# One filling slab of a state-space stage queued behind the stage's last product

## The chip, the cores and the metric

The kernel runs on one core of a Trainium2 chip. The metric is the device time of one execution in microseconds (us). Engines are named as in the profile: PE is TensorE (PEld its weight loads), DVE is VectorE, ACT is ScalarE, POOL is GpSimd, SP is SyncE, which issues the DMAs. All products are of float32 data, split into a high and a low part, so that one logical product is three on PE (high by high, low by high, high by low).

## What is computed

One decoder layer over 1024 tokens of width 1024 with two token mixers side by side, cut here to what matters:

```python
h = rmsnorm(x, norm_w) * (1 + scale) + shift               # scale, shift, gate from c
z_ssm, xbc, dt_raw, q, k, v, z_att, f_logit, g_logit = split(h @ w_in)
# state-space branch: conv and silu on xbc, then 8 chunks of 128 tokens, 16 heads of 64
y = diag(C B^T * L) @ x  +  C @ state  +  d_skip * x         # state runs from chunk to chunk
y_ssm = rmsnorm(y * silu(z_ssm), ssm_norm_w)
# attention branch: 8 heads of 128, causal softmax with a forgetting bias
y_att = softmax(q k^T * s + f_i - f_j) @ v * silu(z_att)
merged = g_ssm * (y_ssm @ w_proj_ssm) + g_att * (y_att @ w_proj_att)
out = rmsnorm(x + gate * (merged @ w_out), final_norm_w)
```

## The kernel before

The kernel is written with a tile framework. The program is traced in source order; then a planner in the compiler lays out a fixed queue for each engine. It steps through a simulated timeline and, whenever an engine is free, gives it the instruction of highest priority whose inputs are planned to be there. Priority is source order, raised for blocks under `tc.high_priority`. Tiles of one tag share a fixed number of buffers (`bufs`); a tile gets its buffer when its first write is placed, and gives it back after its last use. On the chip the queues run as laid out.

The stages around the change:

- **Projection stage** (up to about 500 us of the span): `h` lies in SBUF as `hh`, `hl` (high and low part). Column slabs of `w_in` are multiplied with it and stored to DRAM.
- **State-space stage** (lines 637 to 801, pool `sd`): for each of four groups of heads (`qd`) and each half of the sequence (`hf`), `ssd_half` runs four chunks `c`. A chunk has, on PE, two transposes (L698), three products for the new state (L718), twelve for the part inside the chunk (`yd`, L735) and four for the part from the state (`yo`, L746 and L747). DVE and ACT form the decay matrix and carry the state `st32` from chunk to chunk. After a half, two rows of `y` are finished (L779, L780) and their squares are added into `sacc` (L782 to L785). `ssd_half` has high priority (offset 300).
- **Filling slabs** (`fill`, L762, and `FILL`, L55): parts of the projection that attention needs later, put into this stage so that PE has something to do while the chain of the state waits. They are three slabs of v and seven of q and k (`SPILL`). The list of the last group is `[1, 3, 6, 7, 8]`: `fill[8]` is `qk_spill("k", 5)`, the k of head 5, called **k5** here. A slab is `c_slab` (L115): two weight units, each loaded (L85), cast (L98) and subtracted (L99), then two halves of 24 products (L111 to L113) into one PSUM tile `mm` each. Tag `mm` has three buffers (L74), `wh` and `wl` five each (L92, L95), `wr` four. A half of k5 is read out by L191 into a tile `qt` of tag `ev` (four buffers for the whole kernel, L80), and the slab is stored by L192.
- **End of the stage**: eight products per half of `sacc` with a column of ones (L791) give the sums of squares (`rps`), then L794, L796 (POOL), L798, L800 and a store to `r_scr`. When the last reader of the pool `sd` is done, the pools of attention (`at`, `atp`) take its memory.
- **Attention** (L974 to L1088): `attend(h)` has high priority (offset 1000). The q and k of head 0 are loaded from the spilled ones (L990); those of head 1, **q1** and **k1**, are not spilled. `qk_slab(1)` computes them with `c_slab` into the same three `mm` buffers and reads them out (L980, L981, L985, L986) into tiles of `at`. `u_scaled` (L810) loads, scales and stores the eight rows of y again through `ev` tiles, six of them after head 0. The load of k5 comes with head 5 (L990).
- After that, early products of the state-space branch (L913 to L915, L964 to L966) fill the rest of attention, then the output products follow.

Of the kernel before, what the change touches and what calls it, by code (L numbers as in the profile page):

```python
# [51 lines left out]
WPREP = {1: [('ps', 0)], 2: [('ps', 1)], 3: [('ps', 2)], 6: [('ps', 3), ('pa', 0)], 8: [('pa', 1)], 10: [('pa', 2), ('g', 0)], 12: [('pa', 3), ('g', 2), ('g', 3)], 11: [('g', 1)], 13: [('G', 0)], 15: [('o', 0)], 16: [('o', 1)], 17: [('o', 2)], 18: [('o', 3)]}  # L52
PREP = (6, 1, 0, 0, 0, 0, 0, 0, 1)
APRI, SPRI = 1000, 300
FILL = [[], [0, 2], [4, 5, 9], [1, 3, 6, 7, 8]]  # L55
PAIRS = [(G0 + 4, G0 + 5), (XB0 + 8, XB0 + 9), (G0 + 6, G0 + 7), (XB0, XB0 + 1), (Z0, Z0 + 1), (XB0 + 2, XB0 + 3),
         (Z0 + 2, Z0 + 3), (XB0 + 4, XB0 + 5), (G0 + 8, G0 + 9), (XB0 + 6, XB0 + 7), (G0 + 10, G0 + 11)]
# [8 lines left out]
def build(ctx, tc, t):  # L66
    nc = tc.nc
    V, A, G, PE, SP = nc.vector, nc.scalar, nc.gpsimd, nc.tensor, nc.sync
# [269 lines left out]
    def v_slab(pair, dtf=None):  # L338
        vt = []

        def evac(tb, ps):
            per = ps.shape[1]
            g, i = tb // 4, tb % 4
            if i == 0:
                vt.append(ev("vt")[:, :1024].rearrange("p (i c) -> p i c", i=4))
            A.copy(out=vt[g][:, i:i + per, :], in_=ps[:, :, 0:256])
            if dtf is not None:
                V.tensor_copy(out=dtf[:, tb:tb + per, :], in_=ps[:, :, 256:280])  # L348
            if i + per == 4:
                SP.dma_start(out=v_scr[pair][g], in_=vt[g])  # L350

        if dtf is not None:
            with tc.issue_after(was["last"].ins):
                t_slab([t["w_v0"][u] for u in range(4)], 280, hh, hl, evac)
        else:
            t_slab([t["w_v"][pair - 1, u] for u in range(4)], 256, hh, hl, evac)
# [280 lines left out]
    with tc.tile_pool(name="sd", bufs=1, side="right") as sd, \  # L637
            tc.tile_pool(name="sdp", bufs=1, space=PSUM) as sdp:

        def sp():  # L640
            return sdp.tile([P, 512], F32, tag="sp", bufs=4, name="sp")
# [8 lines left out]
        cl = [sd.tile([P, S], F32R, name=f"cl{g}") for g in range(2)]  # L650
# [12 lines left out]
        for c in range(NC):  # L663
            tk = slice(c * P, (c + 1) * P)
# [5 lines left out]
            if c < NC - 1:  # L670
# [4 lines left out]
                A.copy(out=bt[:, c, 0].rearrange("p (q d) -> p q d", q=2), in_=b4[:, 0::3])  # L675
                A.copy(out=bt[:, c, 1].rearrange("p (q d) -> p q d", q=2), in_=b4[:, 1:3])

        def ssd_half(qd, hf, xs, ys, st32, sn):

            g = qd // 2  # L680
            gs = slice(g * 64, (g + 1) * 64)
            for c in range(4 * hf, 4 * hf + 4):
                tk = slice(c * P, (c + 1) * P)
# [30 lines left out]
                so = sn  # L714
# [22 lines left out]
                if c > 0:  # L737
                    eb = sd.tile([P, 2, P], F32, tag="eb", bufs=2, name="eb")
                    for z in range(2):
                        SP.dma_start(out=eb[z * 64:(z + 1) * 64],  # L740
                                     in_=e_scr[r0:r0 + 4].rearrange("(r two) l -> two r l", two=2)[z:z + 1]
                                     .broadcast_to([64, 2, P]))
                    yo = sp()
                    for i in range(2):
                        ps_ = slice(i * P, (i + 1) * P)
                        PE.matmul(yo[:, ps_], lhsT=so[:, ps_], rhs=ch[g][:, tk], start=True, stop=False)  # L746
                        PE.matmul(yo[:, ps_], lhsT=so[:, ps_], rhs=cl[g][:, tk], start=False, stop=True)  # L747
                    V.tensor_tensor(out=ys[:, :, th], in0=yo[:, 0:256].rearrange("p (r l) -> p r l", r=2), in1=eb,
                                    op=ALU.mult)
                    for z in range(2):  # L750
                        V.tensor_tensor(out=ys[half[z], :, th], in0=yd[z], in1=ys[half[z], :, th], op=ALU.add)
                else:
                    for z in range(2):
                        A.copy(out=ys[half[z], :, th], in_=yd[z])
            return sn

        def qk_spill(n, h):
            evac, store = qk_out(n, h)
            c_slab(t["w_c"], (Q0 if n == "q" else K0) + h, hh, hl, evac)
            store()  # L760

        fill = [lambda p=p: v_slab(p) for p in (1, 2, 3)] + [lambda a=a: qk_spill(*a) for a in SPILL]  # L762
        sacc = sd.tile([P, S], F32, name="sacc")
        for qd in range(4):
            st32, sn = sd.tile([P, 256], F32, tag="st32", bufs=1, name="st32"), None
            for hf in range(2):
                hs = slice(hf * 512, (hf + 1) * 512)
                xs = [sd.tile([P, 512], F32, tag="xs", bufs=5, name="xs") for _ in range(2)]
                for i in range(2):
                    SP.dma_start(out=xs[i], in_=x_scr[2 * qd + i][:, hs])  # L770
                ys = sd.tile([P, 2, 512], F32, tag="ys", bufs=2, name="ys")
                with tc.high_priority(offset=SPRI):
                    sn = ssd_half(qd, hf, xs, ys, st32, sn)
                for i in range(2):
                    j = 2 * qd + i
                    zt = sd.tile([P, 512], F32, tag="zt", bufs=2, name="zt")
                    SP.dma_start(out=zt, in_=z_scr[j][:, hs])
                    y = ys[:, i]
                    V.scalar_tensor_tensor(out=y, in0=xs[i], scalar=dskip[:, j:j + 1], in1=y, op0=ALU.mult, op1=ALU.add)  # L779
                    V.tensor_tensor(out=y, in0=y, in1=zt, op=ALU.mult)  # L780
                    if j == 0:
                        A.activation(out=sacc[:, hs], in_=y, func=AF.Square)  # L782
                    else:
                        A.activation(out=zt, in_=y, func=AF.Square)
                        V.tensor_tensor(out=sacc[:, hs], in0=sacc[:, hs], in1=zt, op=ALU.add)  # L785
                    SP.dma_start(out=u_scr[j][:, hs], in_=y)
            for f in FILL[qd]:
                fill[f]()
        rps = sp()
        for tb in range(8):  # L790
            PE.matmul(rps[:, 2 * tb:2 * tb + 1], lhsT=sacc[:, tb * P:(tb + 1) * P], rhs=ones[:, 0:1],  # L791
                      start=True, stop=True)
# [457 lines left out]
```

## Time and profile before

| what | us |
|---|---|
| median of 3 runs (lowest to highest) | 1224.31 (1223.64 to 1227.98) |
| the profiled execution, its own time | 1224.89 |
| its span in the profile | 1223.2 |
| state-space stage, last product L747 starts | 715.68 |
| first product of attention, L1030 | 729.09 |

The profile's page has the busy time of each engine; the windows view has it for any stretch of time, with the granted clock of PE (1.00 is full speed) and the share of time in which the DMA engines were busy. The timeline view lists instructions in order of their start; in brackets stands the time for which the engine sat idle before one and what ended it.

### The profile page before, as it was taken

Reading aid. Unit: us, or ns where it says so; the run is one execution under the profiler, and the core shown is the slowest. Engines: PE = TensorE matmul, PEld = TensorE weight load, DVE = VectorE, ACT = ScalarE, POOL = GpSimd, SP = SyncE. Lnnn points to the kernel's source line nnn. Section 1 sums busy time; section 2 is a strip of 40 time slices with the busy share of each in tenths; the row PEclk is TensorE's granted clock in tenths of the full one; section 3 lists DMA queues with packets and bytes.
Section 4 is the critical chain, followed back from the end, with each engine's and each line's share of the span. In section 5 each row is a group of like instructions: output and inputs, shape, how many; then the busy total and the mean of one; then the engine's idle time right before and its main releaser. Section 6 shows DMA issues by size and latency. Waiting matters only on the chain.

```text
span 1223.2 us, 18391 instructions
## 1 busy us (share of the span) xinstructions
PE 1162.6 (95%) x6206; PEld 976.3 (80%) x6206; DVE 957.2 (78%) x1950; ACT 626.5 (51%) x1252; POOL 88.3 (7%) x152
## 2 busy tenths in 40 slices
PE   4899999999999999999999989999989998999997
PEld 2788888788877878998987777888877886788876
DVE  6956689788987685589999986664677968989967
ACT  5554444453443334777676633454456644354465
POOL 2000000000000000000000002222322220000001
PEclk9899999999999999999999999999999999999999
DMA  8765543655485665646545658422255526965333
GB/s 351 274 233 184 185 154 93 231 189 189 129 309 167 224 224 200 202 152 223 187 150 186 199 213 294 155 92 73 87 176 195 182 77 239 326 190 182 104 96 147
DMA packets 109018, 228.26 MB, mean 187 GB/s; under 512 B 12362, under 2 KB 20220, under 8 KB 107900
## 3 DMA queue, kind: packets, MB, share of 16 engines
q1 hardware_dynamic: 108924, 227.09, 55.1%
q8 instruction: 49, 0.80, 0.3%
q14 instruction: 45, 0.37, 0.1%
HBM read 159.14 MB, written 67.90 MB: 186 GB/s over the span
## 4 chain that ended last, share of the span: by engine, by line
PE 66%; DVE 15%; DMA 12%; issue 4%; ACT 3%; POOL 1%; SPq 0%; DVEq 0%; POOLq 0%; ACTq 0%
PE pp L497 4%; PE pp L499 4%; PE pp L500 4%; PE pv L1061 4%; PE mm L497 3%; PE mm L499 3%; PE mm L112 3%; PE mm L500 3%; PE mm L113 3%; PE lg L1030 3%; PE mm L111 3%; DMA ab<-a_scr 3%; PE tp L1051 2%; PE mm L915 2%; PE mm L913 2%
## 5 line engine op out<-in xcount | busy, mean ns | idle before, releaser
L98 ACT CAST wh<-wr 128x512 fp32r<-128x512 f32 (+1 forms) x214 | 130.8, 619 | 171.7 <-DMA wr<-w_c 35.0
L99 DVE TENSOR_TENSOR wl<-wr,wh 128x512 fp32r<-128x512 f32 (+1 forms) x214 | 145.5, 686 | 44.9 <-ACT wh L98 44.6
L112 PE MATMUL mm<-hl,wh 128*128 128x512 f32 x288 | 116.4, 404 | 1.9 <-DVE hl L306 1.9
L111 PE MATMUL mm<-hh,wh 128*128 128x512 f32 x288 | 115.7, 406 | 0.1
L113 PE MATMUL mm<-hh,wl 128*128 128x512 f32 x288 | 115.1, 400 | 0.0
L136 PE MATMUL mm<-wh,hh 128*128 128x256 f32 (+1 forms) x256 | 73.8, 289 | 2.4 <-DVE tmp L348 2.4
L137 PE MATMUL mm<-wl,hh 128*128 128x256 f32 (+1 forms) x256 | 74.4, 292 | 0.0
L138 PE MATMUL mm<-wh,hl 128*128 128x256 f32 (+1 forms) x256 | 73.6, 288 | 0.0
L1036 ACT ACTIVATE pr<-pr,sm 128x1024 f32<-128x1024 f32 (+3 forms) x64 | 49.9, 780 | 44.8 <-DVE sm L1035 38.1
L1054 ACT CAST pth<-tp 128x512 fp32r<-128x512 f32 (+1 forms) x80 | 42.5, 542 | 53.5 <-PE tp L1051 43.7
L1031 DVE CUSTOM_DVE_ANT_0 pr<-lg,fb 128x512 f32<-128x512 f32 (+1 forms) x96 | 51.3, 551 | 18.7 <-PE lg L1030 13.2
L112 PEld LDWEIGHTS mm<-hl,wh 128*128 128x128 f32 x288 | 55.0, 191 | 13.2 <-DVE hl L306 3.3
L113 PEld LDWEIGHTS mm<-hh,wl 128*128 128x128 f32 x288 | 54.9, 191 | 10.3
L111 PEld LDWEIGHTS mm<-hh,wh 128*128 128x128 f32 x288 | 54.5, 191 | 10.5 <-ACT hh L305 0.7
L690 ACT ACTIVATE ab<-ab,acs 128x128 f32<-128x128 f32 x128 | 41.2, 391 | 37.7 <-DMA ab<-a_scr 34.1
L1055 DVE TENSOR_TENSOR ptl<-tp,pth 128x512 fp32r<-128x512 f32 (+1 forms) x80 | 49.9, 630 | 10.2 <-ACT pth L1054 9.8
L1039 POOL TENSOR_SCALAR pr<-pr,sm 128x1024 f32<-128x1024 f32 (+3 forms) x64 | 52.2, 816 | 78.2 <-DVE sm L1038 65.4
L98 ACT CAST sh<-sr 128x512 fp32r<-128x512 f32 x57 | 33.9, 619 | 42.3 <-DVE sr L479 31.3
L796 POOL TENSOR_TENSOR fl<-fl,mhalf 128x8 f32<-128x8 f32 x1 | 1.6, 1648 | 699.0 <-DVE fl L794 699.0
L136 PEld LDWEIGHTS mm<-wh,hh 128*128 128x128 f32 x256 | 48.8, 191 | 2.8 <-DVE tmp L348 2.6
L138 PEld LDWEIGHTS mm<-wh,hl 128*128 128x128 f32 x256 | 49.1, 192 | 0.0
L137 PEld LDWEIGHTS mm<-wl,hh 128*128 128x128 f32 x256 | 48.9, 191 | 0.2
(406 smaller groups left out, 3485.5 us busy)
## 6 DMA issues: line engine op xcount, KB each, us to landing
wr<-w_c SPq DMA_DIRECT2D x116, 256.0 KB, 3.7
wa<-w_ada SPq DMA_DIRECT2D x8, 1024.0 KB, 11.4
g_scr<-gt SPq DMA_DIRECT2D x16, 512.0 KB, 4.2
ab<-a_scr SPq DMA_DIRECT2D x32, 256.0 KB, 3.9
gt<-g_scr SPq DMA_DIRECT2D x32, 256.0 KB, 4.0
wr<-w_ps SPq DMA_DIRECT2D x28, 256.0 KB, 2.7
wr<-w_pa SPq DMA_DIRECT2D x28, 256.0 KB, 2.7
wr<-so SPq DMA_DIRECT2D x28, 256.0 KB, 2.7
```

The source lines that it names most:

```text
L98: A.copy(out=hi[:, :n], in_=raw[:, :n])
L99: eng.tensor_tensor(out=lo[:, :n], in0=raw[:, :n], in1=f32(hi[:, :n]), op=ALU.subtract)
L111: PE.matmul(ps, lhsT=hi[:, cs], rhs=xh[k][:, hs], start=(k == 0), stop=False)
L112: PE.matmul(ps, lhsT=hi[:, cs], rhs=xl[k][:, hs], start=False, stop=False)
L113: PE.matmul(ps, lhsT=lo[:, cs], rhs=xh[k][:, hs], start=False, stop=(k == 7))
L136: PE.matmul(o, lhsT=xh[k][:, ts], rhs=hi[:, cs], start=(k == 0), stop=False)
L137: PE.matmul(o, lhsT=xh[k][:, ts], rhs=lo[:, cs], start=False, stop=False)
L138: PE.matmul(o, lhsT=xl[k][:, ts], rhs=hi[:, cs], start=False, stop=(k == 7))
L497: PE.matmul(ps, lhsT=f[0][:, w], rhs=xh[:, hs], start=(first and k == 0), stop=False, skip_group_check=True)
L499: PE.matmul(ps, lhsT=f[0][:, w], rhs=xl[:, hs], start=False, stop=False, skip_group_check=True)
L500: PE.matmul(ps, lhsT=f[1][:, w], rhs=xh[:, hs], start=False, stop=(k == 3), skip_group_check=True)
L1039: G.tensor_scalar(out=pr[:, :n], in0=pr[:, :n], scalar1=sm[:, 1:2], scalar2=0.5, op0=ALU.mult, op1=ALU.mult)
```

## The change

The planner is told that every PE instruction of `fill[8]` (k5) comes behind the last `yo` product of the state-space stage in PE's queue. `last_mm["ssd"]` holds the product traced last (L747 of group 3, second half, chunk 7, second pair); `tc.issue_after` adds for each PE instruction traced in its block an edge to that product: order of issue only, no wait for its result. The loads, casts, subtractions, read-outs and the store of k5 get no such edge. Nothing else changes.

```diff
@@ -52,6 +52,7 @@
 APRI, SPRI = 1000, 300
+KEPT = 8
 FILL = [[], [0, 2], [4, 5, 9], [1, 3, 6, 7, 8]]
@@ -675,6 +676,8 @@
+        last_mm = {}
+
         def ssd_half(qd, hf, xs, ys, st32, sn):
@@ -744,7 +747,8 @@
                         PE.matmul(yo[:, ps_], lhsT=so[:, ps_], rhs=ch[g][:, tk], start=True, stop=False)
-                        PE.matmul(yo[:, ps_], lhsT=so[:, ps_], rhs=cl[g][:, tk], start=False, stop=True)
+                        last_mm["ssd"] = PE.matmul(yo[:, ps_], lhsT=so[:, ps_], rhs=cl[g][:, tk], start=False,
+                                                   stop=True)
@@ -785,7 +789,11 @@
             for f in FILL[qd]:
-                fill[f]()
+                if f == KEPT:
+                    with tc.issue_after(last_mm["ssd"].ins):
+                        fill[f]()
+                else:
+                    fill[f]()
```

## The prediction

> **What bounds the kernel now.** I read the page first, for which engine carries the end, then the windows around the stage's end, then the timelines of PE, DVE, ACT and SP there.
>
> ```profile
> span 1223.2 us, 18391 instructions
> PE 1162.6 (95%) x6206; PEld 976.3 (80%) x6206; DVE 957.2 (78%) x1950; ACT 626.5 (51%) x1252; POOL 88.3 (7%) x152
> PE 66%; DVE 15%; DMA 12%; issue 4%; ACT 3%; POOL 1%; SPq 0%; DVEq 0%; POOLq 0%; ACTq 0%
> ```
>
> PE is busy for 1162.6 of 1223.2 us. The change adds and removes no PE work, so it acts through PE's 60.6 us of idle time and through the clock: a microsecond is lost when PE stands still where it now works, and won back only where it later finds work in what is now an idle stretch. The windows (columns: length, then busy time and count of PE, PEld, DVE, ACT, POOL, then granted clock, DMA share, GB/s) show where idle time lies:
>
> ```profile
> 640.00:703.40 63.40, 59.66 (x377) 49.25 (x377) 59.46 (x145) 41.10 (x100) 0.00 (x0) 1.00 0.61 196
> 703.40:715.90 12.50, 12.37 (x85) 10.18 (x82) 11.60 (x29) 3.07 (x6) 0.00 (x0) 1.00 0.67 228
> 715.90:724.40 8.50, 8.50 (x43) 7.07 (x43) 6.98 (x13) 1.86 (x3) 0.00 (x0) 1.00 0.37 126
> 724.40:770.00 45.60, 39.17 (x201) 32.30 (x200) 30.98 (x61) 18.77 (x33) 11.00 (x15) 0.96 0.77 271
> 770.00:1223.00 453.00, 432.12 (x2236) 362.79 (x2234) 345.40 (x754) 232.09 (x459) 70.80 (x122) 0.99 0.47 155
> ```
>
> From 703.4 to 724.4 PE is never short of work. DVE, with 11.60 of 12.50 us, is the engine that paces the state's chain there. So the gap that a kept slab could fill, from the last product to the sums of squares, is full already. What fills it is in the next fence:
>
> ```profile
> 715.68 0.28 PE L747 MATMUL sp<-cl,sn 128*128 128x128 f32 x1
> 715.80 1.00 PE L791 MATMUL sp<-ones,sacc 128*128 128x1 f32 x8
> 716.66 0.47 PE L111 MATMUL mm<-hh,wh 128*128 128x512 f32 x1
> 716.97 0.39 PE L112 MATMUL mm<-hl,wh 128*128 128x512 f32 x1
> 717.20 0.39 PE L113 MATMUL mm<-hh,wl 128*128 128x512 f32 x1
> ...
> 724.15 0.39 PE L113 MATMUL mm<-hh,wl 128*128 128x512 f32 x1
> 724.38 0.95 PE L791 MATMUL sp<-ones,sacc 128*128 128x1 f32 x8
> ```
>
> Whose products are these? k5's read-outs and stores tell (L191 reads out a half, L192 stores a slab):
>
> ```profile
> 692.36 0.60 ACT L191 ACTIVATE qt<-mm 128x512 f32<-128x512 f32 x1
> 702.77 0.59 ACT L191 ACTIVATE qt<-mm 128x512 f32<-128x512 f32 x1
> 689.30 0.32 SPq L192 DMA_DIRECT2D q_scr<-qt  x1
> 691.66 0.42 SPq L812 DMA_DIRECT2D ut<-u_scr  x1
> 703.39 0.45 SPq L192 DMA_DIRECT2D k_scr<-qt  x1
> ```
>
> q7 is stored at 689.30 and k5, the last spilled slab, at 703.39: k5's two halves were read out at 692.36 and 702.77. So the filling products after 702.4 are q1 and k1, of head 1 of attention. A count on tile `mm` (same columns):
>
> ```profile
> 703.40:715.90 12.50, 9.16 (x36) 6.47 (x36) 0.00 (x0) 0.00 (x0) 1.00 0.67 228
> 715.90:724.40 8.50, 7.74 (x33) 6.13 (x33) 0.00 (x0) 0.00 (x0) 1.00 0.37 126
> 728.21 1.07 ACT L980 ACTIVATE qh<-mm 128x512 fp32r<-128x512 f32 x2
> 731.79 0.49 PE L111 MATMUL mm<-hh,wh 128*128 128x512 f32 x1
> ```
>
> 36 and 33 products, and one triple just before 703.4, are 72 = 3 x 24: q1's two halves and k1's first, one in each of the three `mm` buffers. Then it stops. They can be read out only into attention's tiles, which come with the end of the pool `sd` (L980 at 728.21), and the next filling product is at 731.79. **The reader should see two things**: three buffers are all that attention's slabs can take ahead of time, and a later instruction in the source does take a buffer ahead of an earlier one (the load of `ut`, L812, was issued at 691.66 into a tile of tag `ev`, before k5's own `ev` tile was written at 692.36, though k5 comes first in the source).
>
> **The change part by part.** k5's 48 products lose their place between about 686 and 702.4. They may go behind 715.68. Loads, casts and subtractions of k5's two units stay early (no edge binds them).
>
> *What takes the places.* q1 is ready at that time. Its products move up, then k1's first half: the 72 products of above. From 686 to 715.7 there are 48 + 39 = 87 places, so the 72 are used up about 15 products before the last product, near 709.5. By then all three `mm` buffers hold q1 and k1, which nobody can read out before `sd` closes. **k5 finds no buffer behind the last product**, and PE has no filling until q1 is read out. That is my forecast: the slab that was kept for the gap isn't in the gap.
>
> *What is deferred.* One product takes 0.23 us in a row (716.97 to 717.20), so 48 x 0.23 = 11.1 us of PE work pass from before 724.4 to attention. It is behind attention's own work in priority; its reader, the load for head 5, is far:
>
> ```profile
> 889.95 0.32 SPq L990 DMA_DIRECT2D qt<-k_scr  x1
> ```
>
> *What becomes earlier.* The sums of squares wait for DVE:
>
> ```profile
> 716.55 0.69 DVE L99 TENSOR_TENSOR wl<-wr,wh 128x512 fp32r<-128x512 f32 x1
> 721.03 0.68 DVE L99 TENSOR_TENSOR wl<-wr,wh 128x512 fp32r<-128x512 f32 x1
> 721.63 1.48 DVE L785 TENSOR_TENSOR sacc<-sacc,zt 128x512 f32<-128x512 f32 x2
> ```
>
> `sacc` is complete at 723.11, the products that read it start at 724.38: 1.27 us go, since no filling stands in front. The two subtractions in that tail are for units of later slabs; with k5's two units held, five `wh`/`wl` buffers don't suffice for them, and they drop out of the tail. Both lie between steps of the chain; I count 1.0 of their 1.37 us. The chain before gains at most DVE's idle time, 12.50 - 11.60 = 0.9 us; I take 0.5. Together attention starts 2.8 us earlier (bounds 1.3 and 3.5).
>
> *The clock.* After idle stretches the granted clock falls in this trace:
>
> ```profile
> 724.40:727.50 3.10, 1.11 (x10) 0.92 (x8) 1.23 (x2) 2.14 (x3) 1.65 (x1) 1.00 0.17 70
> 727.50:729.00 1.50, 0.08 (x1) 0.00 (x0) 1.50 (x4) 1.50 (x3) 0.00 (x0) 0.86 0.75 289
> 729.00:731.80 2.80, 2.71 (x7) 2.16 (x8) 2.80 (x4) 0.76 (x2) 0.59 (x2) 0.50 1.00 392
> ```
>
> PE works 1.19 of 4.6 us there and then runs at 0.50. With an empty gap from about 716.7 to 722 the eight records of L791 behind it run at half clock: 0.8 us more (their 0.84 us between starts once again). The slow stretch after 729 is there already and stays. By the Trainium skill, "TensorE: Matmul & The Clock Gate", Part 1, an idle window of about 3.4 us halves the clock, and a busy one of 3.4 us restores it. The trace's 0.50 agrees with the half; were the gap charged one whole slow window, 3.4 / 2 = 1.7 us, an estimate from that page, the sum would end 0.9 us higher.
>
> *What is won back.* The deferred work fills later idle time, if that idle time is for want of filling. Candidates:
>
> ```profile
> 906.69 0.47 PE L111 MATMUL mm<-hh,wh 128*128 128x512 f32 x1
> 923.03 0.51 PE L913 MATMUL mm<-bh,wh 128*128 128x512 f32 x1
> 910.00:920.00 10.00, 6.08 (x24) 4.14 (x24) 7.98 (x26) 5.70 (x12) 3.75 (x5) 0.82 0.97 332
> 1000.00:1020.00 20.00, 17.32 (x120) 15.07 (x119) 10.98 (x33) 9.40 (x22) 6.01 (x12) 1.00 0.12 39
> 1020.00:1040.00 20.00, 18.21 (x75) 13.35 (x73) 19.15 (x32) 10.09 (x18) 0.00 (x0) 1.00 1.02 356
> ```
>
> The hole at 910 to 920 lies between the last slab's products (last L111 at 906.69) and the first early product (L913 at 923.03), while DMA is full (0.97); it moves with the last slab and isn't filled. The end of attention, 1000 to 1020, lacks filling: 2.7 us. From 1020 to 1040 PE waits for loads (DMA 1.02): 1.8 us more. I take both, 4.5. The bounds are nothing and 11.1, all of it, since 724.4 to 1223 has 6.4 + 20.9 us of idle time.
>
> *The rest.* k5's store of 512 KB moves from 703.39 to some 20 us after the slab's new place; on SP it stands among the loads of `ut`, and k5's `ev` tile takes one of four buffers from their cycle. PE waits little for that cycle, so I cost it at nothing; with the cover gone it is one wait as below, 1.0 us.
>
> ```profile
> 768.33 0.36 PE L1061 MATMUL pv<-pth,vh 128*128 128x256 f32 x1 [1.00 <-DVE zg L1064]
> ```
>
> **Sum**: +11.1 - 2.8 + 0.8 - 4.5 = +4.6 us on the profiled execution's own 1224.89 us (span 1223.2 and 1.7 around it). That execution lies 0.6 above the median of 1224.31; put on the median it is 1228.9, say **1229.0**.
>
> **The rivals.**
>
> *Nothing is won back.* The same start, but attention's queue keeps its holes because they are waits for DVE, POOL and loads: 11.1 - 2.8 + 0.8 = +9.1, about 1233.5. For it: between 770 and 900 PE is full, and the holes named above have other waits beside them. It decides from the point where less than 3.0 us is absorbed: then the loss is above 0.5%, 6.1 us, about what a measurement of this kernel can tell from no change.
>
> *The change does what it says.* A buffer is free when the last product is placed (k1's first half not yet begun, or buffers kept for k5), and k5 runs from 715.8 to 727 in place of q1 and k1. Then all 120 products run before attention as now, in another order. `sacc` ready at 723.1 would find eight to sixteen of k5's products in front, +2 to +3.7, unless its products go first; with the tail shorter by 1.0 it is -1 to +3, so 1223 to 1227. Against it: 72 products are fewer than 87 places.
>
> *Faster.* Attention starts 2.8 us earlier, all of k5 is absorbed in the 27.3 us of later idle time, and the planner, which lays out anew all that follows, removes the hole after the last slab (3.9 us in 910 to 920): -2.8 + 0.8 - 3.9 = -5.9, about 1218. For it speaks only the amount of idle time.
>
> **How the numbers follow.** Forecast (some absorbed, +2 to +6) 0.42; little or nothing absorbed (+6 to +11) 0.35; does what it says 0.15; faster, by this or another effect of planning anew, 0.08. Within 0.5% (1218.2 to 1230.4): 0.57; slower by more 0.35; faster by more 0.08. The forecast's own range is 1226 to 1231. The range for 8 in 10 goes from 1221, 3 us below the median among the lower cases, to 1235, the case in which nothing is absorbed and attention starts only 1.3 us earlier (11.1 - 1.3 + 0.8 = +10.6).
>
> **What would show it.** In the changed profile: L191's last read-out after the first L980, not before; 72 products of tile `mm` between k5's old place and the end of the stage; PE idle for some 5 us between L747 and the second L791, and L791 about 2.8 us earlier in the span; the last slab's L111 (now 906.69) some 10 to 30 us later. If L111 products run right behind L747 and L191 reads out before L980, k5 had a buffer and the second rival holds. If PE's idle time after attention's start shrinks by more than 8 us, absorption was underrated; if not at all, the first rival holds.

## The result and the profile after

The changed kernel takes 1238.91 us (median; 1237.66 to 1240.09) against 1225.32 us for the kernel before on the same chip: a ratio of 1.0099, with a 95% interval of 1.0081 to 1.0118. Run again later (label e9_changed_again) it took 1240.31 us against 1223.87, ratio 1.0133 (1.0112 to 1.0154). So it is slower by 13.6 to 16.4 us. The forecast was +4.6 us, with a range that ended at 1235.

The page of the changed kernel, in the order of the lines shown of before, and its windows around the end of the stage (length, then busy time and count of PE, PEld, DVE, ACT, POOL, then granted clock, DMA share, GB/s). Line numbers grow by up to 8 with the change: L750 is the last `yo` product, L799 the sums of squares, L192 k5's read-out, L112 to L114 the slab products, L988 q1's read-out, L1038 attention's first product.

```profile
span 1238.3 us, 18382 instructions
PE 1172.6 (95%) x6206; PEld 985.2 (80%) x6206; DVE 961.5 (78%) x1950; ACT 626.4 (51%) x1252; POOL 87.6 (7%) x152
PE 63%; DVE 17%; DMA 11%; issue 4%; ACT 4%; SPq 1%; POOL 0%; DVEq 0%; POOLq 0%; ACTq 0%
```

```profile
684.00:716.40 32.40, 20.90 (x123) 17.46 (x122) 29.85 (x78) 13.04 (x32) 0.00 (x0) 0.58 0.36 113
716.40:729.20 12.80, 12.80 (x50) 10.27 (x51) 5.96 (x10) 2.50 (x5) 0.00 (x0) 0.86 0.53 169
729.20:770.00 40.80, 40.80 (x205) 34.20 (x204) 27.85 (x53) 16.27 (x27) 7.95 (x12) 1.00 0.85 305
```

The hole isn't behind the last product but ahead of it: from 684 to 716.4 PE stands idle for 11.5 us, and the granted clock there is 0.58. From the same place in the kernel before:

```profile
684.00:715.90 31.90, 31.00 (x208) 25.80 (x207) 29.97 (x77) 15.76 (x36) 0.00 (x0) 1.00 0.63 208
```

85 PE instructions are missing in that stretch. k5, q1 and k1 held 87 places there before (k5's products begin at about 684), and nothing took them. The stage didn't end sooner for it (29.85 and 29.97 us of DVE in both). The timeline of PE, shortened, shows what follows:

```profile
689.44 0.45 PE L749 MATMUL sp<-ch,sn 128*128 128x128 f32 x1 [2.34 <-DVE sn L100]
...
706.83 0.44 PE L749 MATMUL sp<-ch,sn 128*128 128x128 f32 x1 [2.77 <-DVE sn L100]
...
716.19 0.41 PE L750 MATMUL sp<-cl,sn 128*128 128x128 f32 x1
716.40 0.73 PE L112 MATMUL mm<-hh,wh 128*128 128x512 f32 x1
716.93 0.63 PE L113 MATMUL mm<-hl,wh 128*128 128x512 f32 x1
...
728.96 0.39 PE L114 MATMUL mm<-hh,wl 128*128 128x512 f32 x1
729.18 1.84 PE L799 MATMUL sp<-ones,sacc 128*128 128x1 f32 x16
730.88 0.47 PE L112 MATMUL mm<-hh,wh 128*128 128x512 f32 x1
...
742.64 0.40 PE L1038 MATMUL lg<-kh,qh 128*128 128x512 f32 x1
```

The reader should see four things. PE waits for the state (DVE) with nothing else in its queue. k5's 48 products stand exactly where the change says, from 716.40 to 729.2. The sums of squares come behind them, at 729.18 where they were at 724.38. And q1 begins only behind k5, at 730.88, where it was at 702.4. Attention's first product is 13.6 us later (742.64 against 729.09), and this stays: the last output row of attention is stored 14.8 us later (1033.62 against 1018.81), and the span ends 15.1 us later. The stores of attention's output rows, before and then after:

```profile
819.73 0.32 SPq L1065 DMA_DIRECT2D o_scr<-zg  x1
...
1018.81 0.38 SPq L1065 DMA_DIRECT2D o_scr<-zg  x1
```

```profile
834.04 0.32 SPq L1073 DMA_DIRECT2D o_scr<-zg  x1
...
1033.62 0.38 SPq L1073 DMA_DIRECT2D o_scr<-zg  x1
```

### The profile page after: what moved, and what is told of

Its sections match the earlier page's. It is cut to its first block, busy times and chain, and to the rows that moved or that the text cites. A ratio compares the mean times of both kernels' runs of the same rounds, so it can differ in the third digit from the quotient of the medians.

```text
span 1238.3 us, 18382 instructions
## 1 busy us (share of the span) xinstructions
PE 1172.6 (95%) x6206; PEld 985.2 (80%) x6206; DVE 961.5 (78%) x1950; ACT 626.4 (51%) x1252; POOL 87.6 (7%) x152
## 4 chain that ended last, share of the span: by engine, by line
PE 63%; DVE 17%; DMA 11%; issue 4%; ACT 4%; SPq 1%; POOL 0%; DVEq 0%; POOLq 0%; ACTq 0%
PE pp L498 4%; PE pp L500 4%; PE pp L501 4%; PE pv L1069 4%; PE mm L113 4%; PE mm L114 4%; PE mm L112 4%; PE lg L1038 3%; DMA ab<-a_scr 3%; PE mm L498 3%; PE mm L500 3%; PE mm L501 3%; PE tp L1059 2%; DMA wr<-w_c 2%; DVE wl L100 2%
## 5 line engine op out<-in xcount | busy, mean ns | idle before, releaser
L100 DVE TENSOR_TENSOR wl<-wr,wh 128x512 fp32r<-128x512 f32 (+1 forms) x214 | 148.4, 700 | 51.6 <-ACT wh L99 47.5
L114 PE MATMUL mm<-hh,wl 128*128 128x512 f32 x288 | 116.1, 404 | 0.0
L112 PE MATMUL mm<-hh,wh 128*128 128x512 f32 x288 | 116.0, 407 | 0.1
L1039 DVE CUSTOM_DVE_ANT_0 pr<-lg,fb 128x512 f32<-128x512 f32 (+1 forms) x96 | 51.4, 550 | 16.6 <-PE lg L1038 12.9
L114 PEld LDWEIGHTS mm<-hh,wl 128*128 128x128 f32 x288 | 55.4, 193 | 10.6
L112 PEld LDWEIGHTS mm<-hh,wh 128*128 128x128 f32 x288 | 54.8, 192 | 10.7 <-ACT hh L306 0.7
```

The lines of the kernel that those rows point to most:

```text
L100: eng.tensor_tensor(out=lo[:, :n], in0=raw[:, :n], in1=f32(hi[:, :n]), op=ALU.subtract)
L112: PE.matmul(ps, lhsT=hi[:, cs], rhs=xh[k][:, hs], start=(k == 0), stop=False)
L114: PE.matmul(ps, lhsT=lo[:, cs], rhs=xh[k][:, hs], start=False, stop=(k == 7))
L1039: V.tensor_tensor_reduce(out=pr[:, n0:n1], in0=lg[:, :n1 - n0], in1=fb[:, n0:n1], op0=ALU.add, op1=ALU.min, scale=1.0, scalar=BIG, accum_o ...
```

## The experiments

The question was why q1 didn't take the places that k5 left. **Theory A**: the planner hands out the buffers of one tag in source order, so k5's `mm` tile, not yet placed, holds back every later tile of the tag, though buffers are free. **Theory B**: q1 wasn't ready, because k5's two weight units keep two of five `wh` and `wl` buffers. **Theory C**, on where the time goes: the loss is the later sums of squares and the chain behind them, not the PE work left undone. Medians and ratios to the kernel before:

| run | tied | median us | before | ratio (95%) |
|---|---|---|---|---|
| changed | k5 | 1238.91 | 1225.32 | 1.0099 (1.0081 to 1.0118) |
| e1 | k5, in `sp` buffers | 1235.36 | 1226.11 | 1.0079 (1.0051 to 1.0107) |
| e2 | q7 instead | 1246.72 | 1226.11 | 1.0169 (1.0145 to 1.0194) |
| e3 | k5's second half | 1231.37 | 1226.11 | 1.0041 (1.0024 to 1.0057) |
| e4 | k5, behind the sums | 1244.04 | 1226.11 | 1.0148 (1.0114 to 1.0183) |
| e5 | as e1, again | 1234.28 | 1224.5 | 1.0088 (1.0066 to 1.0110) |
| e6 | nothing; q1 spilled | 1224.15 | 1224.5 | 1.0010 (0.9996 to 1.0025) |
| e7 | q1, spilled, in `sp` | 1225.46 | 1224.5 | 1.0004 (0.9989 to 1.0020) |
| e8 | k5, in `sp`, behind the sums | 1234.29 | 1223.87 | 1.0082 (1.0062 to 1.0103) |
| e9 | changed, again | 1240.31 | 1223.87 | 1.0133 (1.0112 to 1.0154) |

**e1: k5 off the tag.**

```diff
-            c_slab(t["w_c"], (Q0 if n == "q" else K0) + h, hh, hl, evac)
+            c_slab(t["w_c"], (Q0 if n == "q" else K0) + h, hh, hl, evac, sp if (n, h) == ("k", 5) else mm_tile)
...
-            ps = mm_tile()
+            ps = bank()
```

> k5 stays tied behind the last product, but its two halves accumulate in two buffers of tag sp (the state-space stage's own) instead of mm. Theory A (buffers of one tag are handed out in source order, so k5's unplaced mm tile blocks q1 and k1, which come later in the source): with k5 off the tag, q1 and k1 fill the places before the last product, PE's granted clock stays at 1.00 there, and the time falls back to 1226 to 1229, 10 us or more below the changed kernel (1238.9). Theory B (q1 was not ready because k5 holds two of the five weight-unit buffers wh and wl): the hole before the last product stays and the time stays at 1237 to 1241.

PE's timeline and windows by stage, in the profile of e1:

```profile
687.62 0.45 PE L113 MATMUL mm<-hl,wh 128*128 128x512 f32 x1
...
705.79 0.39 PE L112 MATMUL mm<-hh,wh 128*128 128x512 f32 x1
709.73 0.30 PE L749 MATMUL sp<-ch,sn 128*128 128x128 f32 x1 [1.06 <-DVE ys L752]
714.03 0.45 PE L749 MATMUL sp<-ch,sn 128*128 128x128 f32 x1 [0.86 <-DVE sn L100]
714.92 0.73 PE L112 MATMUL sp<-hh,wh 128*128 128x512 f32 x1
```

```profile
684.00:716.00 32.00, 27.90 (x184) 23.40 (x183) 29.48 (x75) 11.93 (x28) 0.00 (x0) 0.92 0.35 113
```

With nothing altered but the PSUM tag of k5, the tie still in force and the unit buffers the same, q1 and k1 fill the places from 687 on and run out near 706. That refutes B and is what A says. Up to the last product this is the course that the prediction had given to the change itself: the 72 products run out ahead of it. Behind it k5 has its buffers in `sp` and runs, where the prediction had it find none. But the time didn't fall by 10 us: the kernel is still 9.3 us above the kernel before of its chip, where the changed kernel is 13.6 and 16.4 above. The expectation of 1226 to 1229 was missed, and the granted clock was 0.92, not 1.00.

**e5** is the same kernel again, since e1's profiled execution (1228.02 us) lay apart from its timed ones (1235.31 to 1236.08).

> The kernel with k5 in sp buffers once more, because its profiled execution (1228.0 us) and its four timed ones (1235.3 to 1236.1) lay apart. Theory A gives 1226 to 1229 from the profiled trace, in which q1 and k1 fill the places. If the time is 1234 to 1237 again, something that this trace doesn't show costs 7 us in most executions, and the profile should be of one of these.

It took 1234.28 us, 9.8 above the kernel before of its chip, so 1234 to 1235 is this kernel's median, and e1's profile was of a quick execution. In e5's profile (1232.6 us) these places differ from the kernel before:

```profile
728.86 1.84 PE L799 MATMUL sp<-ones,sacc 128*128 128x1 f32 x16
734.46 0.77 PE L1038 MATMUL lg<-kh,qh 128*128 128x512 f32 x1 [1.50 <-DVE rr L808]
775.12 0.39 PE L1069 MATMUL pv<-pth,vh 128*128 128x256 f32 x1 [2.26 <-ACT pth L1062]
776.50 0.39 PE L1069 MATMUL pv<-ptl,vh 128*128 128x256 f32 x1 [0.87 <-DVE ptl L1063]
```

```profile
684.00:716.00 32.00, 27.84 (x185) 23.29 (x184) 29.90 (x75) 13.01 (x30) 0.00 (x0) 0.95 0.39 123
```

There are 4.2 us of idle ahead of the last product (0.9 before the change), attention's first product is 5.4 us later, and two new waits of 3.1 us together stand at 775. What each of them is worth wasn't separated. Why executions of this one kernel differ by up to 8 us stays open; those of the kernel before, on the same chip as e5, go from 1221.0 to 1230.4.

**e2: q7 held instead of k5** (`KEPT = 7`).

> q7, the slab before k5, is tied behind the last product instead of k5. Theory A: k5 and q1 come after q7 in the source and stop too; 48 more products (11.1 us) leave the stage, and the time is 1244 to 1251. Theory B: q7 holds two unit buffers, k5's two and one of q1 are there, so k5 fills the places and the time is 1236 to 1241. Theory C (the loss is only that the sums of squares come later, behind 48 products): the sums come behind 96 products, so about 11 us more as well; A and C then differ in whether the hole starts earlier.

It took 1246.72 us. In its profile the last filling product ahead of the hole starts at 665.91 (in the changed kernel's at 684.01), the casts of weight units (ACT) stop at 671.4, and the state's products are alone until 711.88; all of q7 and k5 runs after that, from 712.09 on:

```profile
671.38 0.61 ACT L99 CAST wh<-wr 128x512 fp32r<-128x512 f32 x1
719.41 0.60 ACT L192 ACTIVATE qt<-mm 128x512 f32<-128x512 f32 x1 [2.40 <-PE mm L114]
```

```profile
665.91 0.39 PE L114 MATMUL mm<-hh,wl 128*128 128x512 f32 x1
...
711.88 0.41 PE L750 MATMUL sp<-cl,sn 128*128 128x128 f32 x1
712.09 0.73 PE L112 MATMUL mm<-hh,wh 128*128 128x512 f32 x1
...
735.88 1.84 PE L799 MATMUL sp<-ones,sacc 128*128 128x1 f32 x16
```

k5 isn't tied here. By the count of the five unit buffers it was ready: the last two casts (666.17 and 671.38) are k5's second unit and q1's first, beside two of q7. Still it stopped with q7. A's 1244 to 1251 holds, and B's 1236 to 1241 was missed. The hole starts 18 us sooner than in the changed kernel, and the run is 20.6 us above the kernel before of its chip, not 13.6 or 16.4.

**e3: half of k5 held.**

```diff
+            if hold is not None and hf == 1:
+                with tc.issue_after(hold):
+                    c_half(hf, units, xh, xl, ps)
+            else:
+                c_half(hf, units, xh, xl, ps)
```

> Only k5's second half (24 products) is tied; the first half is free. Theory A: 24 products return to their places before the last product, and after it 24 k5 products end before the sums are ready, with q1 behind them; 63 products (14.6 us) are deferred instead of 72 plus a later end, less about 7.6 us of idle time that they fill: 1230 to 1234. Theory C (late sums): the sums come at about 723, as before the change, so 1224 to 1227.

```profile
684.00:716.00 32.00, 22.56 (x140) 19.22 (x139) 29.51 (x76) 11.45 (x27) 0.00 (x0) 0.69 0.46 152
716.00:730.00 14.00, 14.00 (x70) 11.59 (x69) 7.86 (x12) 5.46 (x8) 1.94 (x2) 0.99 0.64 198
720.61 0.95 PE L800 MATMUL sp<-ones,sacc 128*128 128x1 f32 x8
722.43 0.95 PE L800 MATMUL sp<-ones,sacc 128*128 128x1 f32 x8
```

1231.37 us. The sums are even 1.95 us earlier than in the kernel before (722.43 against 724.38), and still it is 5 us slower: A's 1230 to 1234 holds, and C's 1224 to 1227 was missed. So the loss isn't the sums' own place. But the chain behind them didn't keep their lead: attention's first product comes at 734.77, 5.7 us later than in the kernel before. Beside the hole of 9.4 us ahead of the last product, that late start remains as a possible cause.

**e4: k5 behind the sums**, traced after them and tied to their last product.

```diff
+        with tc.issue_after(last_mm["ssd"].ins):
+            fill[KEPT]()
```

(`last_mm["ssd"]` is here the last product of `sacc` with the ones.)

> k5 is traced after the sums of squares and tied behind their last product (L796 here) instead of the last yo product. The sums then come about 6 us earlier than in the changed kernel, and PE is empty from the last yo product to the sums, about 6 us more. Theory A (what counts is PE work not done while the stage waits): 1239 to 1245, no better than the changed kernel. Theory C (what counts is the late sums and the chain behind them): 1232 to 1235.

```profile
725.12 1.87 PE L796 MATMUL sp<-ones,sacc 128*128 128x1 f32 x8 [4.08 <-DVE sacc L789]
735.28 0.60 ACT L192 ACTIVATE qt<-mm 128x512 f32<-128x512 f32 x1 [11.13 <-PE mm L114]
747.23 0.61 PE L1037 MATMUL lg<-kh,qh 128*128 128x512 f32 x2
```

1244.04 us: the sums come 4 us sooner than in the changed kernel, and it is no faster, as A expected (1239 to 1245). But this doesn't settle C. The chain behind the sums came later, not sooner: ACT waits 11.13 us for k5's first half, attention's first cast stands behind that read-out in its queue (738.34, in the changed kernel 731.06), and attention's first product is 4.6 us later than there (747.23 against 742.64). **e8** makes the same comparison with k5 off the tag, against e5.

> k5 in two sp buffers, as in e1 and e5, but traced after the sums of squares and tied behind their last product. The same 120 products fill up to attention; only their order against the sums differs. In e5 the sums start at 728.9, 4.5 us later than before the change; here they come at about 722 to 724, PE is empty for some 6 us ahead of them, and k5 covers the wait for POOL and the pool change behind them (about 5 us empty before). Theory A (only work not done while the stage waits counts): the 6 us of emptiness and the 5 us of cover nearly cancel, 1232 to 1236, as e5. Theory C (late sums are what e5 still loses): 1224 to 1228.

```profile
723.74 1.86 PE L796 MATMUL sp<-ones,sacc 128*128 128x1 f32 x8 [4.08 <-DVE sacc L789]
744.68 0.63 PE L1037 MATMUL lg<-kh,qh 128*128 128x512 f32 x2
```

1234.29 against 1234.28 us for e5: sums 5.1 us sooner, the same time. Here too attention starts later, by 10.2 us (744.68 against 734.46), with about 24 more filling products done before it. So sooner sums alone bring nothing; what a sooner start of the whole chain would bring, e4 and e8 don't show. **e9** ran beside e8, for the changed kernel's own time on that chip:

> The changed kernel unaltered, beside e8 on the same chip, so that differences of some us between the variants are read against the spread of one and the same program: 1237 to 1241.

It took 1240.31 us, so on one chip e8 is 6 us under the changed kernel.

**e6 and e7: a slab that blocks nobody.** q1 becomes a spilled slab, read out to DRAM, so that it gives its buffers back; in e7 it is also tied behind the last product, in two `sp` buffers, with k5 free.

```diff
-SPILL = (("q", 0), ("k", 0), ("k", 2), ("k", 4), ("q", 7), ("k", 5), ("k", 6), )
+SPILL = (("q", 0), ("k", 0), ("k", 2), ("k", 4), ("q", 7), ("k", 5), ("k", 6), ("q", 1))
-FILL = [[], [0, 2], [4, 5, 9], [1, 3, 6, 7, 8]]
+FILL = [[], [0, 2], [4, 5, 9], [1, 3, 6, 7, 8, 10]]
```

> Nothing is tied. q1 becomes an eighth spilled slab, traced after k5, so that it is read out to DRAM and gives its mm buffers back; k1 and the first half of q2 can then fill behind it. Theory A (three mm buffers, handed out in source order, limit what fills the end of the stage): filling lasts past the sums of squares, PE's idle time between 724 and 732 (about 5 us in the kernel before, and about 1.2 us at half clock behind it) is filled, and the time is 1219 to 1223. If the spill's own loads and splits cost as much, 1224 to 1227.

> As e6, but q1 is tied behind the last yo product and accumulates in two sp buffers; k5, k1 and the first half of q2 stay free in mm. This is the change's aim without its blocking: the tied slab blocks nobody, the places before the last product are filled by k5 and k1, q1 stands in the gap, the sums behind it. Theory A: 1220 to 1225, with the sums at about 727 as the price against e6. Theory C (late sums count): 3 us or more above e6.

The windows of e6, then those of e7:

```profile
684.00:716.00 32.00, 31.18 (x207) 25.85 (x205) 30.11 (x76) 14.56 (x33) 0.00 (x0) 1.00 0.48 157
716.00:730.00 14.00, 14.00 (x71) 11.67 (x70) 8.35 (x13) 6.58 (x10) 1.65 (x1) 1.00 0.79 274
```

```profile
684.00:716.00 32.00, 30.95 (x205) 25.74 (x204) 29.87 (x76) 13.43 (x30) 0.00 (x0) 1.00 0.40 128
716.00:730.00 14.00, 14.00 (x71) 11.72 (x70) 8.13 (x13) 6.87 (x11) 1.65 (x1) 1.00 0.79 265
737.98 0.39 PE L1038 MATMUL lg<-kh,qh 128*128 128x512 f32 x1
```

PE is full through the stage's end in both, with the clock at 1.00. 1224.15 and 1225.46 us: neither differs from the kernel before, and the gain that A expected (1219 to 1223 for e6, 1220 to 1225 for e7) didn't show. So a tie as such costs nothing measurable where filling is left for the places ahead of it; and the empty 5 us behind the sums, once filled, brought nothing that can be measured either; what the spill's extra loads and splits took of a gain wasn't separated. These two runs also say what e3, e4 and e8 can't: attention starts 8.6 and 8.9 us later here than in the kernel before (737.73 and 737.98), with some 55 more filling products done before it, and nothing is lost. A late start of attention is thus no loss by itself, where the work done before it makes up for it. No version was found that beats the kernel before.

## Why the prediction was wrong

- **The bound** was read rightly: PE work that isn't done in the stage is what counts. From 684 to 715.9 the chain of the state is paced by DVE, and taking 85 PE instructions away didn't shorten it in this trace: last product at 716.19 against 715.68, where a gain of 0.5 us was counted.
- **The step that failed** is "q1 is ready at that time. Its products move up". q1 was ready and didn't move. The first sign for it was misread: the load of `ut` at 691.66, ahead of k5's read-out at 692.36, was taken to show that a later tile of a tag takes a buffer first. But these are times on the chip; what counts is when the planner placed the two, and its own times aren't in the profile. With k5 tied, the `ut` load went to 721.00, just ahead of k5's first read-out at 723.81, and the loads of head 0's q and k behind it from 695.60 to 721.51:

```profile
721.00 0.46 SPq L820 DMA_DIRECT2D ut<-u_scr  x1
723.81 0.60 ACT L192 ACTIVATE qt<-mm 128x512 f32<-128x512 f32 x1 [2.49 <-PE mm L114]
```

  So the loads into tag `ev` were held back too. e1 and e2 show the order for tag `mm`: take k5 off the tag and q1 runs; tie q7 and k5 stops. With that, the next step failed as well: the `mm` buffers weren't full of q1 and k1, and k5 did find one behind the last product.
- **The deferred work** was mis-sized by that step. From 684 to the end of the sums 120 filling products ran before the change and 48 after it: 72 x 0.23 = 16.6 us, not 11.1. The sums end 5.6 us later (730.9 against 725.3; L799 from 729.18, L791 from 724.38), where 2.8 us earlier was counted: k5's own products stand in front. Together 22.2 us.
- **What is won back**: the idle time after attention's start. From 724.4 to 770 the kernel before had 6.4 us, which the prediction left out of what it took as won back; now PE is full from 716.4 to 770 and at full clock from 720, so those 6.4 us and about 1.2 us of half clock are gone. 22.2 - 7.6 = 14.6, against 15.1 measured in the span. The 4.5 us from 1000 to 1040 were not won: attention's rows come 14.3 us later at 834 and 14.8 at 1033.6.
- **The clock**: half clock was foreseen for the eight records of L791, 0.8 us. It came in the stage itself, where the last product is only 0.5 us later at a granted clock of 0.58 (whether a gain is hidden there isn't shown), and in k5's first eight products, at 0.43 instead of 0.23 us apart: 1.6 us.
- **The rivals**: "does what it says" was right about the place of k5 and wrong about the time, since it let q1 run as before. Where q1 does run (e1, e5), the time is still 9.3 and 9.8 us above the kernel before, and this rival had -1 to +3: it named the 15 places that the 72 products leave empty, but gave them no price (in e5 PE idles 4.2 us ahead of the last product, 0.9 before), and it didn't foresee attention's start 5.4 us later. "Nothing is won back" had the right sign from other terms. The 87 places of the prediction are those from 684 on; from 686, where it began them, the trace has 80.

## What to carry to other kernels

Work that is tied back isn't only itself late: every tile behind it in the source that shares its tag can be late with it, buffers free or not. Before tying something, look at what follows it in the same tag, and give the tied work buffers of its own and other work enough for the places that it leaves. With buffers of its own alone (e1, e5, e8) the loss was still 9 to 10 us; with both (e7) none could be measured. A gap that the profile shows as full can't be won by moving filling into it.

## What the runs showed of the hardware

In the changed kernel the granted clock stayed at half for 27 us, though PE was busy for two thirds of them, with idle stretches in between. The windows view (length, then PE busy):

```profile
686.00:689.40 3.40, 0.52 (x4) 0.20 (x2) 2.89 (x7) 3.25 (x9) 0.00 (x0) 0.96 0.66 219
689.40:716.40 27.00, 18.38 (x100) 15.53 (x101) 25.00 (x65) 8.35 (x20) 0.00 (x0) 0.50 0.29 94
699.50:704.10 4.60, 4.50 (x31) 4.21 (x31) 4.46 (x12) 2.03 (x5) 0.00 (x0) 0.50 0.10 29
716.40:719.90 3.50, 3.50 (x9) 2.75 (x10) 3.18 (x6) 0.00 (x0) 0.00 (x0) 0.50 0.02 5
719.90:729.00 9.10, 9.10 (x41) 7.36 (x40) 2.78 (x5) 2.45 (x4) 0.00 (x0) 1.00 0.73 234
```

It fell after 3.4 us with 0.52 us of work, stayed at 0.50 for 27 us at 18.38 us of (slowed) work with no idle stretch over 2.8 us, and came back at 719.9, when PE had worked without a gap for 4.4 us (since 715.52, the first of the stage's last four products). The Trainium skill, "TensorE: Matmul & The Clock Gate", Part 1, gives at least one busy window of about 3.4 us for the return; the 4.4 us agree with that. But such a length alone didn't suffice here: from 699.56 to 704.06 PE worked 4.5 us without a gap as well, and the clock stayed at 0.50. In e9's profile, of the same kernel, the same stretch (698.45 to 702.91) did bring it back, at about 702.7. What made the difference isn't shown. A long gap isn't needed for the fall either: in e1's profile the clock fell at about 711.0, with no idle stretch over 1.1 us in the 10 us ahead of that.
